# A fused transformer block on one Trainium2 core: whole float32 products for weight tiles without a place, residual sums in single steps, gate columns made later

## The chip, the cores and the metric

The kernel runs on one NeuronCore of a Trainium2 chip. The core has five engines that run side by side, each with its own queue of instructions, worked off in order: TensorE (PE, matrix products; its weight loads are shown as PEld), VectorE (DVE, elementwise work and sums along a row), ScalarE (ACT, functions and copies), GpSimd (POOL) and SyncE (SP, which here only issues transfers). Engines wait for one another through semaphores. The metric is the device time of one execution in microseconds (us), the median of several runs.

## The reference

The block has 256 tokens of 2048 channels and three sublayers: a SwiGLU layer, a mixer (mLSTM heads beside a gated linear recurrence), and a second SwiGLU layer. Each is followed by a residual sum and a layer norm, and preceded by a norm that is modulated with a scale and a shift computed from a conditioning vector:

```python
y = _swiglu(modulate(x, 0), ffn1_w13[l], ffn1_w2[l])
x = _layer_norm(ALPHA * x + FFN_WEIGHT * gate[:, 0, None, :] * y, ln_g[l, 0], ln_b[l, 0])
u = modulate(x, 1)
proj = u @ w_in[l] + b_in[l]
...
x = _layer_norm(ALPHA * x + gate[:, 1, None, :] * y, ln_g[l, 1], ln_b[l, 1])
y = _swiglu(modulate(x, 2), ffn2_w13[l], ffn2_w2[l])
x = _layer_norm(ALPHA * x + FFN_WEIGHT * gate[:, 2, None, :] * y, ln_g[l, 2], ln_b[l, 2])
```

`modulate(x, s)` is a layer norm without affine part, times `1 + scale`, plus `shift`. In the mLSTM, the input and forget gate of four heads give, per token, a running sum of log forget gates and a running maximum; the attention weights of a head are `exp` of differences of these rows. All inputs are float32.

## The kernel before

**Products in three parts.** A float32 product is made of three products in the type fp32r, which TensorE takes faster: every operand is split into a rounded part (hi) and the rest (lo), and hi·hi, lo·hi and hi·lo are summed in PSUM. For a weight tile (128 x 2048, 1 MB, loaded by SP into one of four `raw` buffers) `split` (line 88) makes hi with a cast on ACT (line 95) and lo with a subtraction on DVE (line 97), into one of three hi/lo buffers. `stat_w` (lines 266 to 268) uses the weight as the stationary operand, `mov_t` (lines 277 to 279) as the moving one with 512 columns; activations stand transposed in `uh` and `ul`, 16 blocks of 128 channels by 256 tokens.

**Order.** A planner (the tile framework) orders each engine's queue from a modelled timeline and sets the semaphores. Instructions issued through `V`, `A`, `G` and `T` (class `Pinned`, line 111; all of them are recorded at line 120) keep the order in which the program gives them on DVE, ACT, POOL and PE; all others the planner may move.

**Boundary (line 321).** Between two sublayers the tokens are worked in two tiles of 128 (t = 0, 1). `products(t)` makes the last products of the old sublayer into PSUM tiles `tl`. `take(t, n)` is the residual sum for 512 channels on DVE: product with the gate (`gy`), sum into `x`, row statistics. `norm(t)` is a generator: eight steps on DVE for the layer norm (with row sums), with a square on ACT (`junk`) for each of the last four, then the statistics of the next norm (`tot`, the root on POOL, `nbn` on ACT). `front(t)` makes the next sublayer's input: `n_of` normalises 512 channels, `turned` transposes them on PE into `tu`, `u_of` applies scale and shift (three columns on ACT, one on DVE) and splits the result into `uh` and `ul`, `mov_t` multiplies it with four weight tiles `fw[0..3]` of the next sublayer (`o` after the first boundary, `fg` after the second). `ready` names the tiles of `fw` that find a place (hi/lo buffers or spare slots) before the boundary; the others (`late`) are split in eight or four pieces between the steps of t = 0, hi on ACT, lo on POOL (`late_split`, line 412). At the first boundary (`ffn` of sublayer 0, called at line 1030) tile 3 is late and t = 1 has four residual steps; at the second (end of `mixer`, line 1008) tiles 2 and 3 are late and each t has one.

**Gates (line 804).** In the mixer the projections run over tiles of `w_s`: one tile for the gate rows, 1 to 8 for the recurrence's input (`xr`), 9 to 16 for its output gate (`gg`). `gates()`, called after tiles 1 and 2, makes from the gate rows on DVE a chain of small steps (4 x 256) in the slot `ggt`; its results `gs` and `mt` overwrite two of these rows. `gate_cols()`, called after tile 8, transposes them on PE into `pcol` (lines 819, 820) and copies them to `gcol` and `emc` for the heads. The output gate `gg` is written over the same slot from tile 9 on, by the evacuation at line 759. DVE meanwhile runs the convolution (lines 832 to 836), one product and sum per conditioning tile (line 173, loads `ada`) and the splits `ls`. `rg_gates` (line 838) and `recurrence` (line 848) follow after tiles 12 and 14.

Of the kernel before, what the change touches and what calls it, by code (L numbers as in the profile page):

```python
# [16 lines left out]
P = 128  # L17
# [34 lines left out]
def block_kernel(ctx: ExitStack, tc: tile.TileContext, a: dict, out: bass.AP):  # L52
# [254 lines left out]
    def scaled_by(mv, r, nm):  # L307

        b = sm.tile([P, 1], F32, tag="nb", name="nb" + nm)
        A.mul(b, mv, -1.0)  # L310
        A.activation(b, b, AF.Copy, scale=r)
        return b

# [7 lines left out]
    def boundary(s, ps, hls, order, mm, sts, following):  # L321
# [7 lines left out]
        if following:  # L329
            tiles, nm, ready, in_slots = following  # L330
            fw = [load(tiles[k], f"{nm}{k}", spare if k in in_slots else None) for k in range(4) if k in ready]
        g, b = ln_rows(s)
        if following:
            fw += [load(tiles[k], f"{nm}{k}", None) for k in range(len(fw), 4)]
            late = [k for k in range(4) if k not in ready]
            sb = sm.tile([P, 1], F32, tag="sb", bufs=1, name=f"sb{s}")
# [14 lines left out]
        def low_ahead(k):  # L351
            fw[k] = split(fw[k], nc.scalar, V)

        def norm(t):
# [9 lines left out]
            for n, c in enumerate(cs):  # L364
                if following:
# [3 lines left out]
                    A.activation(junk, x[:, t, c], AF.Square, bias=sb, accum_out=sq[:, 1, n:n + 1])  # L369
# [4 lines left out]
            if following:  # L374
                tot = sm.tile([P, 4], F32, tag="tot", bufs=2, name=f"tot{s}{t}")
                V.tensor_reduce(tot[:, 0:2], sq, op=ALU.add, axis=mybir.AxisListType.X)
                V.tensor_scalar_mul(tot[:, 0:2], tot[:, 0:2], 1.0 / D)
                V.tensor_add(tot[:, 2:3], tot[:, 0:1], sb)

                V.scalar_tensor_tensor(tot[:, 3:4], tot[:, 2:3], tot[:, 2:3], tot[:, 1:2], op0=ALU.mult,  # L380
                                       op1=ALU.subtract)
                r = rstd_in_order(tot[:, 3:4], f"n{s}{t}", -1.0)
                mrb[t] = tot[:, 0:1], r, scaled_by(tot[:, 0:1], r, f"n{s}{t}")
                yield

        def n_of(t, n, k):
            m, r, nb = mrb[t]
            if k == 0:
                V.tensor_scalar(n[:, cs[k]], x[:, t, cs[k]], m, r, op0=ALU.subtract, op1=ALU.mult)
            else:  # L390
                A.activation(n[:, cs[k]], x[:, t, cs[k]], AF.Identity, bias=nb, scale=r)
# [7 lines left out]
        def u_of(t, pt, k):  # L399

            tk = slice(t * P, (t + 1) * P)
            u = sm.tile([P, 4, P], F32, tag="u", bufs=2, name=f"u{s}{t}_{k}")
# [9 lines left out]
        def late_split(k, part):  # L412

            raw, name, _ = fw[k]
            if part == 0:
                lates[k] = [wp.tile([P, 2048], F32R, tag=w, bufs=3, name=w[0] + name) for w in ("hi", "lo")]
            hi, lo = lates[k]
            c = cs[part]
            A.copy(hi[:, c], raw[:, c])
            G.tensor_sub(lo[:, c], raw[:, c], hi[:, c].bitcast(F32))  # L420

        def takes(t, ns):
            for n in ns:
                take(t, n)
                yield
# [6 lines left out]
        def late_pieces():  # L432
            for k in late:
                for part in range(4):
                    late_split(k, part)
                    if part == 3:
                        fw[k] = lates[k]
                    yield

        def front(t, between):  # L440
            n = slot(f"n{s}{t}")[:, 0:D]
            pss.append(bank(f"{nm}{t}"))
            n_of(t, n, 0)
            n_of(t, n, 1)
            pt = [turned(t, n, 0), turned(t, n, 1)]
            for k in range(4):
                between(k)
                u_of(t, pt[k], k)
                if k < 2:
                    n_of(t, n, k + 2)  # L450
                if k:
                    mov_t(pss[t], fw[k - 1], uh, ul, (k - 1) * 4, t, k == 1, False)
                if k < 2:
                    pt.append(turned(t, n, k + 2))
            mov_t(pss[t], fw[3], uh, ul, 12, t, False, True)

        mrb, lates, pss = {}, {}, []
# [14 lines left out]
        A.mul(sb, sb, -1.0 / D)  # L472
        many = len(order[1]) > 1
        other = chain(takes(1, order[1]), norm(1))
        one = norm(0)
        pieces = late_pieces()
        run(one, 8)
        if many:
            run(other, 1)
        run(one)  # L480
        if many:
            run(other, 1)

        def beside(k):
            run(pieces, (0, 2, 2, 0)[k] if len(late) == 1 else 2)
            run(other, (1, 1, 3, 3)[k] if many else (1, 3, 3, 3)[k])

        front(0, beside)
# [636 lines left out]
```

## Time and profile before

| | |
|---|---|
| median of 3 runs | 2036.04 us (2035.77 to 2036.55) |
| the profiled execution | 2036.97 us, span 2035.2 us |
| clock granted to TensorE, mean | 0.981 of full |
| HBM read | 509.22 MB, 251 GB/s over the span |
| first boundary | 801 to 849 us of the span |
| gate columns | 923 to 942 us |
| second boundary | 1236 to 1292 us |

The span is the time between the first and the last instruction of the profiled execution. A profile row of the timeline is: start in us, length in us, engine, line, operation, output and inputs, shapes, count; in brackets the idle time of that engine before it, and what ended it. A row of a group gives count, busy time and mean ns of one, then idle time before. In the waits view a row is engine, line, what it waited for, total us, times, longest.

### The profile page before, as it was taken

The page shows a single profiled execution, that of the slowest core. Times are in us where ns is not written, and L with a number is a line of the kernel's source. Part 1 is how long each engine was busy: PE and PEld are TensorE (multiplying, and loading weights), DVE is VectorE, ACT ScalarE, POOL GpSimd, SP SyncE. Part 2 cuts the span into 40 slices and gives each one's busy share as a digit, 9 for nine tenths or more (in the row PEclk, how much of TensorE's full clock was granted, in tenths as well). Part 3 has the DMA queues.
Part 4 walks back from the last instruction along what each step waited for, and adds up shares of the span by engine and source line. Part 5 has one row for each costly group of instructions (what it writes and reads, how often), then busy time and mean ns, then how long its engine had stood idle before and what let it go on. Part 6 is the DMA issues. An engine that isn't in the chain of part 4 may idle for free.

```text
span 2035.2 us, 30179 instructions
## 1 busy us (share of the span) xinstructions
PE 1952.9 (96%) x13068; PEld 1797.4 (88%) x13068; DVE 1425.5 (70%) x1335; ACT 838.0 (41%) x794; POOL 51.3 (3%) x71
## 2 busy tenths in 40 slices
PE   7899999999999998897999997999999999999997
PEld 6899998799899886697999885899899899899985
DVE  7998898877877757686886886555555544544656
ACT  5433344433334344543744344433433433334340
POOL 0000000000000001100000123000000000000000
PEclk8999999999999999998999998999999999999999
DMA  9998898988988754485687673466666655555552
GB/s 374 349 346 300 307 331 317 349 334 338 358 340 316 264 203 158 159 308 206 237 302 289 223 273 124 170 224 247 237 239 249 227 184 179 189 178 178 187 193 100
DMA packets 72710, 513.27 MB, mean 252 GB/s; under 512 B 8449, under 2 KB 8577, under 8 KB 10881
## 3 DMA queue, kind: packets, MB, share of 16 engines
q1 hardware_dynamic: 70848, 507.54, 67.1%
q10 hardware_dynamic: 1728, 3.80, 0.6%
q8 instruction: 102, 1.67, 0.3%
q14 instruction: 32, 0.25, 0.0%
HBM read 509.22 MB, written 2.10 MB: 251 GB/s over the span
## 4 chain that ended last, share of the span: by engine, by line
PE 86%; DVE 8%; issue 2%; ACT 2%; DMA 2%; POOL 0%; DVEq 0%; SPq 0%; POOLq 0%; ACTq 0%
PE pv L266 6%; PE pv L267 6%; PE pg L268 6%; PE pg L266 6%; PE pv L268 6%; PE pg L267 6%; PE py L278 6%; PE py L279 6%; PE py L277 6%; PE pj L266 2%; PE pj L268 2%; PE pj L267 2%; DVE x L120 2%; PE tl L278 2%; PE tl L279 2%
## 5 line engine op out<-in xcount | busy, mean ns | idle before, releaser
L173 DVE CUSTOM_DVE_ANT_0 ada<-ada,scb,badac 128x2048 f32<-128x2048 f32 x144 | 337.8, 2348 | 31.7 <-DMA ada<-in_w_ada 29.9
L97 DVE TENSOR_TENSOR lw<-rw,hw 128x2048 fp32r<-128x2048 f32 x80 | 183.1, 2290 | 134.2 <-ACT hw L95 134.2
L268 PE MATMUL pg<-uh,lg 128*128 128x256 f32 x960 | 271.8, 283 | 0.0
L268 PE MATMUL pv<-uh,lv 128*128 128x256 f32 x960 | 271.8, 283 | 0.0
L266 PE MATMUL pg<-uh,hg 128*128 128x256 f32 x960 | 271.7, 283 | 0.0
L266 PE MATMUL pv<-uh,hv 128*128 128x256 f32 x960 | 271.7, 283 | 0.0
L267 PE MATMUL pv<-ul,hv 128*128 128x256 f32 x960 | 271.7, 283 | 0.0
L267 PE MATMUL pg<-ul,hg 128*128 128x256 f32 x960 | 271.7, 283 | 0.0
L95 ACT CAST hw<-rw 128x2048 fp32r<-128x2048 f32 x80 | 152.5, 1909 | 214.8 <-PE py L279 63.0
L97 DVE TENSOR_TENSOR lv<-rv,hv 128x2048 fp32r<-128x2048 f32 x68 | 155.7, 2290 | 113.0 <-ACT hv L95 112.9
L95 ACT CAST hv<-rv 128x2048 fp32r<-128x2048 f32 x68 | 129.6, 1906 | 212.6 <-PE pg L267 83.4
L97 DVE TENSOR_TENSOR lg<-rg,hg 128x2048 fp32r<-128x2048 f32 x60 | 137.4, 2291 | 102.1 <-ACT hg L95 102.1
L278 PE MATMUL py<-lw,hth 128*128 128x512 f32 x512 | 203.5, 398 | 2.1 <-DVE lw L97 2.1
L279 PE MATMUL py<-hw,htl 128*128 128x512 f32 x512 | 201.7, 394 | 0.0
L277 PE MATMUL py<-hw,hth 128*128 128x512 f32 x512 | 197.1, 395 | 0.0
L95 ACT CAST hg<-rg 128x2048 fp32r<-128x2048 f32 x60 | 114.3, 1905 | 173.0 <-PE pv L267 115.5
L266 PEld LDWEIGHTS pg<-uh,hg 128*128 128x128 f32 x960 | 183.8, 191 | 0.4
L267 PEld LDWEIGHTS pg<-ul,hg 128*128 128x128 f32 x960 | 183.8, 191 | 0.3
L268 PEld LDWEIGHTS pv<-uh,lv 128*128 128x128 f32 x960 | 183.9, 192 | 0.0
L266 PEld LDWEIGHTS pv<-uh,hv 128*128 128x128 f32 x960 | 183.9, 192 | 0.0
L267 PEld LDWEIGHTS pv<-ul,hv 128*128 128x128 f32 x960 | 183.9, 192 | 0.0
L268 PEld LDWEIGHTS pg<-uh,lg 128*128 128x128 f32 x960 | 183.8, 191 | 0.0
(397 smaller groups left out, 4376.4 us busy)
## 6 DMA issues: line engine op xcount, KB each, us to landing
ada<-in_w_ada SPq DMA_DIRECT2D x144, 1024.0 KB, 5.4
rw<-in_w SPq DMA_DIRECT2D x80, 1024.0 KB, 4.8
rg<-in_w SPq DMA_DIRECT2D x60, 1024.0 KB, 5.0
rv<-in_w SPq DMA_DIRECT2D x60, 1024.0 KB, 4.8
rra<-in_w_r SPq DMA_DIRECT2D x48, 1024.0 KB, 5.5
rs<-in_w_s SPq DMA_DIRECT2D x32, 1024.0 KB, 4.8
rwo<-in_w_out SPq DMA_DIRECT2D x16, 1024.0 KB, 4.8
ro<-in_w_vo SPq DMA_DIRECT2D x8, 1024.0 KB, 4.7
```

What stands on the lines that cost most here:

```text
L95: act.copy(cut(hi, w), like(raw[:, w], hi))
L97: low.tensor_sub(cut(lo, w), like(raw[:, w], lo), cut(hi, w).bitcast(F32))
L120: self.last = getattr(self.engine, op)(*args, **kw)
L173: nc.vector.tensor_tensor_reduce(raw, raw, scb, 1.0, badac[:, s, j, kt:kt + 1], ALU.mult, ALU.add, adac[:, s, j, kt:kt + 1])
L266: nc.tensor.matmul(ps, hi[:, w], uh[:, k0 + j, :], start=st, stop=False)
L267: nc.tensor.matmul(ps, hi[:, w], ul[:, k0 + j, :], start=False, stop=False)
L268: nc.tensor.matmul(ps, lo[:, w], uh[:, k0 + j, :], start=False, stop=sp)
L277: nc.tensor.matmul(o, acth[:, k0 + j, tk], cut(hi, w), start=first and j == 0, stop=False)
L278: nc.tensor.matmul(o, acth[:, k0 + j, tk], cut(lo, w), start=False, stop=False)
L279: nc.tensor.matmul(o, actl[:, k0 + j, tk], cut(hi, w), start=False, stop=last and j == 3)
```

## The change

1. At a boundary the splits of all `ready` tiles are issued before the first residual sum (before, some stood between the sums). The first boundary's tiles are loaded and split in the order 0, 2, 1.
2. `take` yields after each of its three steps, so that `norm` and `take` of the other token tile can be run in single steps; how many steps stand where is written anew (4 per block of t = 0).
3. The statistics after the norm take one DVE step less, and ACT makes the negative mean; a product `sbs` is added.
4. `u_of` uses ACT for all four columns. For a late tile the u of t = 0 is kept whole in float32 in columns of `n0` that are free, and multiplied with the raw weight tile in float32 (`whole_t`: four products of 512 columns). The late weight is split (ACT, DVE) during t = 1, and the whole u is split at the end.
5. The order around the second token tile is new: its first transposes are issued before the last products of t = 0.
6. `gs` and `mt` are written to rows of the slot `misc`, and `gate_cols` is called after tile 14, ahead of `recurrence`; its transposes are pinned.

```diff
-            fw = [load(tiles[k], f"{nm}{k}", spare if k in in_slots else None) for k in range(4) if k in ready]
+            fw = {k: load(tiles[k], f"{nm}{k}", spare if k in in_slots else None) for k in ready}
...
             V.tensor_mul(gy, ps[t, n], gate[:, cs[n]])
+            yield
             V.tensor_add(x[:, t, cs[n]], x[:, t, cs[n]], gy)
+            yield
             V.bn_stats(sts[t][:, n, :], x[:, t, cs[n]])
+            yield
...
-                V.tensor_scalar_mul(tot[:, 0:2], tot[:, 0:2], 1.0 / D)
-                V.tensor_add(tot[:, 2:3], tot[:, 0:1], sb)
+                V.tensor_scalar(tot[:, 2:3], tot[:, 0:1], 1.0 / D, sb, op0=ALU.mult, op1=ALU.add)
...
-                if j < 3:
-                    A.activation(u[:, j, :], pt[:, j * P:(j + 1) * P], AF.Identity, bias=h, scale=m)
-                else:
-                    V.tensor_scalar(u[:, j, :], pt[:, j * P:(j + 1) * P], m, h, op0=ALU.mult, op1=ALU.add)
+                A.activation(u[:, j, :], pt[:, j * P:(j + 1) * P], AF.Identity, bias=h, scale=m)
+            if not whole:
+                split_u(t, u, k)
...
+        def whole_t(ps, raw, u, last):
+
+            for j in range(4):
+                nc.tensor.matmul(ps, u[:, j, :], raw[:, cs[j]], start=False, stop=last and j == 3)
...
-        ahead = list(ready)
-        for i, n in enumerate(order[0]):
-            while ahead and (len(order[0]) == 1 or i == len(order[0]) // 2 or len(ahead) > 2):
-                low_ahead(ahead.pop(0))
-            take(0, n)
+        for k in ready:
+            fw[k] = split(fw[k], nc.scalar, V)
+        run(takes(0, order[0]))
...
+        run(one, 8)
+        run(other, many)
+        run(one)
+        run(other, many)
...
+        un = {k: n0[:, cs[k - 2]].rearrange("p (a b) -> p a b", b=P) for k in late}
+        n_of(0, n0, 0)
+        n_of(0, n0, 1)
+        pt = {}
+        pt[0] = turned(0, n0, 0)
+        pt[1] = turned(0, n0, 1)
...
+        def first(k):
+            if k in late:
+                whole_t(ps0, fw[k][0], un[k], k == 3)
+            else:
+                mov_t(ps0, fw[k], uh, ul, k * 4, 0, k == 0, k == 3)
...
+        for k in range(4):
+            run(other, 4)
+            u_of(0, pt[k], k, un.get(k))
+            if k < 2:
+                n_of(0, n0, k + 2)
+            if k:
+                first(k - 1)
+            if k < 2:
+                pt[k + 2] = turned(0, n0, k + 2)
         run(other)
-        front(1, lambda k: None)
+        n_of(1, n1, 0)
+        n_of(1, n1, 1)
+        pt[0] = turned(1, n1, 0)
+        first(3)
+        pt[1] = turned(1, n1, 1)
+        rest = list(late)
+        for k in range(4):
+            u_of(1, pt[k], k)
+            if k < 2:
+                n_of(1, n1, k + 2)
+            if rest:
+                fw[rest[0]] = split(fw[rest[0]], A, V)
+                rest.pop(0)
+            if k:
+                mov_t(ps1, fw[k - 1], uh, ul, (k - 1) * 4, 1, k == 1, False)
+            if k < 2:
+                pt[k + 2] = turned(1, n1, k + 2)
+        for k in late:
+            split_u(0, un[k], k)
+        mov_t(ps1, fw[3], uh, ul, 12, 1, False, True)
...
-        fc, gs, mx, mt = z4, ig, q4, fg
+        fc, mx = z4, q4
...
+        gs, mt = misc[0:4, 768:768 + S], misc[0:4, 1792:1792 + S]
...
-                nc.tensor.transpose(pcol[:, t * 4:t * 4 + 4], gs[:, t * P:(t + 1) * P], ident[0:4, 0:4])
-                nc.tensor.transpose(pcol[:, 8 + t * 4:12 + t * 4], mt[:, t * P:(t + 1) * P], ident[0:4, 0:4])
+                T.transpose(pcol[:, t * 4:t * 4 + 4], gs[:, t * P:(t + 1) * P], ident[0:4, 0:4])
+                T.transpose(pcol[:, 8 + t * 4:12 + t * 4], mt[:, t * P:(t + 1) * P], ident[0:4, 0:4])
...
-        proj(1, 8, xr, {0: gates, 6: gate_cols})
+        proj(1, 8, xr, {0: gates})
...
-        proj(9, 8, gg, {2: rg_gates, 4: recurrence})
+        proj(9, 8, gg, {2: rg_gates, 4: lambda: (gate_cols(), recurrence())})
...
-    ffn(0, a["w13_1"], a["w2_1"], start, (a["w_vo"][8:12], "o0", (0, 1, 2), (2,)))
+    ffn(0, a["w13_1"], a["w2_1"], start, (a["w_vo"][8:12], "o0", (0, 2, 1), (2,)))
```

More of the change, by code (lines that the diff above doesn't have):

```diff
@@ L304, in scale_x @@
             A.mul(x[:, t, :], x[:, t, :], ALPHA)
[L307 to L312, printed above, removed]
     def rstd_in_order(var, nm, sign=1.0):
@@ L330, in boundary @@
             tiles, nm, ready, in_slots = following
-            fw = [load(tiles[k], f"{nm}{k}", spare if k in in_slots else None) for k in range(4) if k in ready]
+            fw = {k: load(tiles[k], f"{nm}{k}", spare if k in in_slots else None) for k in ready}
         g, b = ln_rows(s)
         if following:
-            fw += [load(tiles[k], f"{nm}{k}", None) for k in range(len(fw), 4)]
             late = [k for k in range(4) if k not in ready]
-            sb = sm.tile([P, 1], F32, tag="sb", bufs=1, name=f"sb{s}")
+            fw.update((k, load(tiles[k], f"{nm}{k}")) for k in late)
+            sbt = sm.tile([P, 2], F32, tag="sb", bufs=1, name=f"sb{s}")
+            sb, sbs = sbt[:, 0:1], sbt[:, 1:2]
         def products(t):
```

73 lines of the change are left out of this document (21 added, 52 removed).

## The prediction

> **What bounds the kernel now.** First the page and the waits of TensorE (engine, line, what it waited for: total us, times, longest).
>
> ```profile
> PE 1952.9 (96%) x13068; PEld 1797.4 (88%) x13068; DVE 1425.5 (70%) x1335; ACT 838.0 (41%) x794; POOL 51.3 (3%) x71
> PE 86%; DVE 8%; issue 2%; ACT 2%; DMA 2%; POOL 0%; DVEq 0%; SPq 0%; POOLq 0%; ACTq 0%
> PE pcol L819 <- DVE gg L810: 13.8, 1, 13.8
> PE tu L120 <- ACT n L120: 10.7, 4, 3.2
> PE fg L277 <- ACT uh L120: 8.6, 3, 4.2
> PE tu L120 <- DVE n L120: 7.9, 3, 5.4
> PE o L277 <- ACT uh L120: 2.6, 2, 1.7
> ```
>
> TensorE is busy 96% of the span and carries 86% of the chain, so only its own idle time can be won. The five longest waits are all in code that the diff touches: the gate columns (13.8 us, once) and the transposes and first products of the two boundaries. The next view is busy time by stage (stretch: length, busy us of PE, PEld, DVE, ACT, POOL, clock), then TensorE's groups inside the two boundaries (the last column is idle time before the group and its releaser).
>
> ```profile
> 801.20:846.50 45.30, 30.19 (x117) 23.21 (x117) 30.11 (x54) 29.03 (x61) 9.76 (x14) 0.81 0.21 73
> 923.00:937.00 14.00, 0.16 (x2) 0.14 (x1) 13.75 (x24) 2.59 (x3) 0.00 (x0) 0.66 0.68 232
> 1235.90:1291.70 55.80, 40.95 (x152) 31.41 (x153) 26.80 (x40) 31.20 (x61) 13.48 (x12) 0.82 0.26 95
> L120 PE MATMUL tu<-ident,n 128*128 128x128 f32 x32 | 6.5, 353 | 12.5 <-DVE n L120 7.7 <-ACT n L120 4.8
> L120 PE MATMUL tu<-ident,n 128*128 128x128 f32 x32 | 5.5, 308 | 6.1 <-ACT n L120 5.9 <-DVE n L120 0.3
> L277 PE MATMUL fv<-hfv,uh 128*128 128x512 f32 x8 | 3.0, 392 | 0.0
> 846.07 0.39 PE L278 MATMUL o<-sl,uh 128*128 128x512 f32 x1
> 846.30 0.40 PE L279 MATMUL o<-sh,ul 128*128 128x512 f32 x1
> 822.28 0.63 PE L277 MATMUL o<-sh,uh 128*128 128x512 f32 x1
> 822.70 0.63 PE L278 MATMUL o<-sl,uh 128*128 128x512 f32 x1
> ```
>
> The first boundary loses 12.5 us before its transposes and 2.6 before its products (o), 15.1 us idle; the second 6.1 and 8.6 (fg), 14.7. On top, after a gap the 512-column products start every 0.42 us (822.28 to 822.70) and not every 0.23 (846.07 to 846.30), with the clock at 0.81 and 0.82 of full.
>
> **Part 1, the gate columns.** Rows in order of time (start, length, engine):
>
> ```profile
> 922.63 0.28 PE L267 MATMUL pj<-ul,hs 128*128 128x256 f32 x1
> 922.75 0.28 PE L268 MATMUL pj<-uh,ls 128*128 128x256 f32 x1
> 926.33 2.27 DVE L97 TENSOR_TENSOR ls<-rs,hs 128x2048 fp32r<-128x2048 f32 x1
> 936.87 0.27 PE L819 MATMUL pcol<-ident,gg 4*128 4x4 f32 x1 [13.84 <-DVE gg L810]
> 937.76 0.41 DVE L813 TENSOR_TENSOR gg<-gg 4x256 f32<-4x256 f32 x1
> 937.87 0.41 PE L266 MATMUL pj<-uh,hs 128*128 128x256 f32 x1
> 938.08 0.41 PE L267 MATMUL pj<-ul,hs 128*128 128x256 f32 x1
> 947.98 2.29 DVE L97 TENSOR_TENSOR ls<-rs,hs 128x2048 fp32r<-128x2048 f32 x1 [5.63 <-ACT hs L95]
> 962.54 1.90 ACT L95 CAST hs<-rs 128x2048 fp32r<-128x2048 f32 x1 [3.82 <-PE pj L267]
> 979.74 1.90 ACT L95 CAST hs<-rs 128x2048 fp32r<-128x2048 f32 x1
> 983.55 2.28 DVE L97 TENSOR_TENSOR ls<-rs,hs 128x2048 fp32r<-128x2048 f32 x1
> 992.40 3.73 PE L144 MATMUL adag<-ident,adac 128*128 128x128 f32 x32
> ```
>
> Tile 8's last product starts at 922.75, the first transpose at 936.87: DVE delivers gs 14 us late. Behind that transpose stand the products of tile 9, although the split of tile 11 (926.33) is done by 928.6. Moved behind tile 14, the four transposes read rows that are final at 938.2 (937.76 + 0.41), long before. The move removes 13.84 us idle and the slow restart: some 18 products at 0.21 us, not 0.12, 1.7 us. Together **15.5 us**. What is late next: tile 9 now runs 922.9 to 928.6 (48 products of 0.12 = 5.76), tile 12 is due at 940.2. Its split stood at 947.98 only because its cast waited behind emc on ACT; in DVE's queue it follows the gate chain, 938.2 + 2.29 = 940.5, so 0.3 us of wait comes back. The evacuations of tiles 9 and 10 overwrite ig and fg, so ACT waits for gs until 936.8, some 2 us that its lead of three tiles hides. Copy gcol and exponential emc move with the transposes and queue before the recurrence. There cover is thin: between the casts at 962.54 and 979.74 ACT has 17.2 us of sigmoids and exponentials, three tiles of TensorE (17.3), and the split behind it ends at 985.8, 0.8 us before tile 16 starts (it ends at 992.40, where the next group begins, so it starts at 986.6). If emc waits there, TensorE pays: 0 to 5 us. The scratch rows cost no instruction. I take **-14.5** (-9 to -16).
>
> **Part 2, the first boundary (801 to 849).**
>
> ```profile
> 781.67 0.69 DVE L120 TENSOR_TENSOR gy<-tl,gate 128x512 f32<-128x512 f32 x1 [5.21 <-PE tl L279]
> 786.55 2.48 DVE L120 TENSOR_TENSOR lo<-ro,ho 128x512 fp32r<-128x512 f32 x4
> 788.95 2.49 DVE L120 TENSOR_TENSOR sl<-ro,sh 128x512 fp32r<-128x512 f32 x4
> 806.62 1.97 PE L120 MATMUL tu<-ident,n 128*128 128x128 f32 x8 [5.40 <-DVE n L120]
> 837.49 0.62 ACT L120 CAST uh<-u 128x512 fp32r<-128x512 f32 x1 [0.48 <-DVE u L120]
> 838.74 1.13 ACT L120 ACTIVATE u<-tu,adac 128x128 f32<-128x128 f32 x3
> 1248.98 1.75 DVE L120 SCALAR_TENSOR_TENSOR x<-x,rsp,ln_b 128x512 f32<-128x512 f32 x1
> 799.20 0.74 DVE L120 SCALAR_TENSOR_TENSOR x<-x,rsp,ln_b 128x512 f32<-128x512 f32 x1
> 962.89 0.59 PE L844 MATMUL pr<-xc,wax 128*128 128x256 f32 x2
> 963.32 0.59 PE L843 MATMUL pr<-xc,wax 128*128 128x256 f32 x2
> ```
>
> (a) *Splits first.* DVE idles 5.21 us ahead of 781.67, and the two 2.5 us splits at 786.55 and 788.95 stand between the residual sums. Put ahead of them they fill the idle time (the third ends near 784.3, after its cast), and the sums run through: the norm starts 3 us earlier. (b) *Single steps.* Two whole takes (three steps of 0.7) stood before and after the row sums of tile 0; now one step each: 2 us. Both together bring the transposes from 806.62 to about 801.4, just behind the last product at 801.2: the 5.40 us gap goes. One scalar step of DVE (0.2 us) goes too; the new product sbs is one ACT step under TensorE's products. (c) *u on ACT alone.* Three columns take 1.13 us, so four 1.5; DVE's fourth column and two handovers go (the cast at 837.49 waited 0.48). Cast and next normalised block take 1.25 more (837.49 to the next u at 838.74), so a block costs ACT 2.8, as much as the 12 products it feeds (12 x 0.23 = 2.8): ACT becomes the pace. (d) *The late tile whole.* The early POOL subtractions go, which cost DVE a doubling (1.75 against 0.74 for one form). Four float32 products replace twelve: a float32 product of 256 columns takes 0.43 (962.89 to 963.32), so 512 columns 0.86 and four 3.4 us, 0.6 more than 2.8. Its split moves to the second block's u, 2.2 us on ACT, 2.5 on DVE, and the late u's cast to the end. Nothing runs on POOL but the square roots.
>
> In order, each engine's queue as the code writes it: transposes 801.4; a gap of 2.4 for u, cast and next block; products of blocks 0 to 2 without a gap to 816.0; two squares of token tile 1 (0.7 each, as all 512-column steps here) delay the late u on ACT to 817.1 (gap 1.1); float32 products to 820.5; second token tile's transposes 820.9, a gap of 2.4, then ACT-paced products to 838.3 (839.3 if the planner puts the float32 products behind those transposes). Idle 6.3 us against 15.1, and one slow restart of about 3. Before, product 846.30 plus tile 3 of token tile 1 (2.8) ends at 849.3. The gain is 10 to 11; a cast of the next weight tile (1.9 on ACT) can fall into the chain: **-10** (-4 to -12).
>
> **Part 3, the second boundary.** One residual step only, so (a) gives nothing and the start stays near 1235.9. Two tiles are late, 4 x 2 float32 products: +1.3 us. POOL's share, and with it DVE's doubled steps, goes. But the code puts a square of token tile 1 ahead of block 1's u, and the statistics of token tile 1 ahead of the two late u: ACT waits 3.0 us for the first and ends the late u near 1252.5 and 1254.0. Gaps of 2.4, 1.7, 1.6 and 2.4 us stay (8 us against 14.7), and restarts stay slow. My queue ends the products at 1275.0 at full clock and 1278.7 with 4 us of 0.42 us starts after each gap over 1.5. Before, they ended with the stretch above, at 1291.5, with a fv tile of 24 products (three groups of 8, 5.6 us) run ahead: 1285.9. Gain 7.2 to 10.9, **-8** (-2 to -11).
>
> [...]
>
> **Sum.** -14.5 - 10 - 8 = -32.5. The profiled execution took 2036.97 (span 2035.2 and 1.8 around it), 0.9 over the median 2036.04: 2004.5 there, **2004** as a median, 1.6% less.
>
> **Rivals.** A, *the gate wait comes back elsewhere*: DVE is busy 13.75 of the 14 us and later must split tiles, copy gcol and run the recurrence in 15 us less; or the transposes are planned early again and wait for mt. For it: the 0.8 us margin; against: DVE's idle at 947.98. 5 to 15 us return: 2009 to 2019, say 2014, 0.17. B, *the clock holds* through the short gaps: parts 2 and 3 come at their full-clock ends, 11 and 10.9: 2000, 0.08. [...] C, *ACT starves the boundaries*: casts of the next tiles and squares sit ahead of u, half of parts 2 and 3 is lost, +9: 2013, 0.10. D, *the raw buffers bind*, the slower side:
>
> ```profile
> rs<-in_w_s SPq DMA_DIRECT2D x32, 1024.0 KB, 4.8
> ```
>
> wax holds one of the four raw buffers until the recurrent gates run and ada tiles another; a load starts only when DVE has done with an earlier tile. If DVE lags so far that one weight tile at a time goes round, load, cast and split in series (4.8 + 1.9 + 2.3 = 9.0 us) replace the 5.76 of its products, 3.2 more per tile. From eleven tiles on the kernel is slower than before; over the 16 tiles from tile 9 through the v projection it is 52 - 32.5, 2055, 0.04. Against it: no wait of TensorE is put down to a load in that stage. E, *the gains are all cover*: TensorE's idle only moves to the following stage: 2036, 0.03.
>
> **How the numbers follow.** Forecast 0.58 (1997 to 2010), A 0.17, B 0.08, C 0.10, E 0.03, D 0.04. The bounds of the three parts taken together, -39 to -15, are 1997 to 2021; they take in A, B and C, and a little below goes to clock and planner: 1995 to 2021, with about 0.13 left out. About 0.2% (4 us) is what a measurement tells from no change: faster 0.93, same 0.03, slower 0.04.
>
> **What would show it.** Part 1: no wait at the transposes, tile 9 straight behind tile 8, pcol after tile 14. Part 2: sums running from 784, transposes near 801, under 7 us of idle to the end of the products. Part 3: three or four gaps of 1.5 to 2.5 us, ACT waiting for the first square. Float32 products at 0.86 us. It is wrong if TensorE waits for ls or lv between 923 and 1040, if the whole products run far over 0.9 us, or if casts break ACT's chain.

## The result, and the profile after

The changed kernel took 2001.79 us (median of 4 runs, 2001.11 to 2003.39), the kernel before, beside it on the same chip, 2036.24 us (4 runs, 2035.77 to 2036.55). The ratio is 0.9832, 95% interval 0.9815 to 0.9849: 34.45 us less, against 32 forecast. The profiled execution has a span of 1999.9 us against 2035.2. Of all executions reported below one, of the changed kernel run again, was slow (2431.24 us at a mean granted clock of 0.726); the ratios leave it out.

First the page of the changed kernel: busy time by engine, and the shares of the chain that ended last.

```profile
PE 1944.2 (97%) x13056; PEld 1785.9 (89%) x13056; DVE 1414.0 (71%) x1327; ACT 843.8 (42%) x812; POOL 36.2 (2%) x59
PE 89%; DVE 6%; ACT 3%; issue 1%; DMA 0%; POOL 0%; DVEq 0%; SPq 0%; ACTq 0%
```

TensorE's share of the chain went from 86 to 89%, DVE's from 8 to 6%: the waits for DVE went, while the work stayed. The waits of TensorE in the changed kernel (engine, line, what it waited for: total us, times, longest):

```profile
PE tu L120 <- ACT n L120: 7.1, 3, 2.4
...
PE fv L277 <- ACT hfv L95: 2.3, 1, 2.3
PE fg L415 <- ACT n L120: 2.3, 1, 2.3
...
PE fv L278 <- DVE lfv L97: 1.6, 2, 1.1
PE tu L120 <- DVE n L120: 1.5, 2, 0.9
PE o L415 <- ACT n L120: 1.3, 1, 1.3
...
PE fg L277 <- ACT uh L120: 1.0, 1, 1.0
```

The 13.8 us for the gate rows are gone, and so are the 5.4 us before the first boundary's transposes. What is left in the boundaries is mostly named ACT: in the rows shown TensorE waits 14.0 us for it (normalised blocks, u, a split) and 3.1 us for DVE. In order of time, TensorE's rows of the first boundary that had idle time before them (start, length, line, tile, in brackets the idle time and its releaser), and the four gate transposes:

```profile
800.66 1.25 PE L120 MATMUL tu<-ident,n 128*128 128x128 f32 x8 [0.59 <-DVE n L120]
804.28 0.66 PE L120 MATMUL tu<-ident,n 128*128 128x128 f32 x4 [2.37 <-ACT n L120]
815.13 3.70 PE L415 MATMUL o<-ro,n 128*128 128x512 f32 x8 [1.31 <-ACT n L120]
819.77 1.25 PE L120 MATMUL tu<-ident,n 128*128 128x128 f32 x8 [0.94 <-DVE n L120]
823.39 1.11 PE L120 MATMUL tu<-ident,n 128*128 128x128 f32 x4 [2.37 <-ACT n L120]
833.74 0.50 PE L278 MATMUL po<-lo,uh 128*128 128x512 f32 x1 [1.08 <-DVE lo L97]
953.64 0.41 PE L120 MATMUL pcol<-ident,misc 4*128 4x4 f32 x4
```

The transposes of the first boundary start at 800.66 and not at 806.62, 0.59 us behind the last products. The gate transposes carry no bracket: TensorE comes to them without a wait. The second boundary, same view:

```profile
1209.20 1.25 PE L120 MATMUL tu<-ident,n 128*128 128x128 f32 x8
1212.82 1.12 PE L120 MATMUL tu<-ident,n 128*128 128x128 f32 x4 [2.37 <-ACT n L120]
1218.57 0.50 PE L277 MATMUL fg<-sh,uh 128*128 128x512 f32 x1 [0.99 <-ACT uh L120]
1224.53 3.70 PE L415 MATMUL fg<-rfg,n 128*128 128x512 f32 x8 [2.25 <-ACT n L120]
1241.73 0.73 PE L277 MATMUL fv<-hfv,uh 128*128 128x512 f32 x2 [2.27 <-ACT hfv L95]
1244.05 0.80 PE L278 MATMUL fv<-lfv,uh 128*128 128x512 f32 x1 [1.07 <-DVE lfv L97]
```

**Where the time came from.** Two executions of the changed kernel differ by a microsecond or two as a whole, those of the kernel before by up to five, so the parts are read from stages: the time between the starts of two TensorE groups that every run has. Stage 1 runs from the first conditioning product `adag` (627 to 629 us) to the first boundary's transposes; stage 2 from there to the `adag` products behind tile 16 (992.40 before), and holds the rest of the first boundary and the gate columns; stage 3 on to the second boundary's transposes; stage 4 from there to the transposes `th` of the second SwiGLU layer (1309.3 before).

| us | stage 1 | stage 2 | stage 3 | stage 4 |
|---|---|---|---|---|
| before | 178.4 | 185.8 | 243.7 | 73.1 |
| changed | 173.6 | 164.9 | 243.6 | 64.8 |
| difference | -4.8 | -20.9 | -0.1 | -8.3 |

Together that is -34.1. Another -1.2 us was there at `adag` already (628.2 before, 627.0 after), though TensorE's order is the same in both kernels up to the first boundary's transposes: runs of the same code spread from 627.0 to 628.8 there, so these 1.2 us are chance.

Stage 2 has a mark inside, the first product of the gate rows, `pif` (its rows before and after: shortest, median and longest in ns, then first and last start):

```profile
L266 PE MATMUL pif<-uh,hif x16: 277/283/283, 871.0 to 876.4; 128*128 128x256 f32 x16
```

```profile
L266 PE MATMUL pif<-uh,hif x16: 278/283/283, 860.2 to 865.6; 128*128 128x256 f32 x16
```

Up to it, in the rest of the first boundary, 64.4 us became 59.6 (-4.8); behind it, with the gate columns, 121.4 became 105.3 (-16.0).

### The profile page after: what moved, and what is told of

Same layout as the page of the kernel before. It is cut to its first block, busy times and chain, and to the rows that moved or that the text cites. A ratio compares the mean times of both kernels' runs of the same rounds, so it can differ in the third digit from the quotient of the medians.

```text
span 1999.9 us, 30155 instructions
## 1 busy us (share of the span) xinstructions
PE 1944.2 (97%) x13056; PEld 1785.9 (89%) x13056; DVE 1414.0 (71%) x1327; ACT 843.8 (42%) x812; POOL 36.2 (2%) x59
## 3 DMA queue, kind: packets, MB, share of 16 engines
q1 hardware_dynamic: 70848, 507.54, 68.6%
## 4 chain that ended last, share of the span: by engine, by line
PE 89%; DVE 6%; ACT 3%; issue 1%; DMA 0%; POOL 0%; DVEq 0%; SPq 0%; ACTq 0%
PE pv L266 6%; PE pg L268 6%; PE pv L267 6%; PE pg L266 6%; PE pv L268 6%; PE pg L267 6%; PE py L278 6%; PE py L279 6%; PE py L277 6%; PE pj L266 3%; PE pj L267 3%; PE pj L268 3%; PE tl L278 2%; PE tl L277 2%; PE tl L279 2%; PE rg L268 2%
```

## The experiments

Twelve kernels, three rounds each with the kernel before beside them (the last two five). The table gives the median, the ratio to the kernel before, and the stages; a dot stands for the value of the changed kernel within 0.1 (stage 3 was 243.6 to 243.8 in all). The stages are those of one profiled execution each.

| run | us | ratio, 95% interval | stage 1 | stage 2 | stage 4 |
|---|---|---|---|---|---|
| gate columns alone | 2019.32 | 0.9924 (0.9909 to 0.9938) | 178.4 | 171.3 | 68.6 |
| boundaries alone | 2015.85 | 0.9909 (0.9894 to 0.9923) | . | 179.5 | 64.6 |
| rows kept, columns early | 2012.80 | 0.9893 (0.9878 to 0.9908) | . | 176.5 | 63.8 |
| u first | 2003.06 | 0.9845 (0.9829 to 0.9862) | . | 166.6 | 62.9 |
| fourth column on DVE | 2011.71 | 0.9882 (0.9868 to 0.9897) | . | 168.7 | 69.8 |
| splits between the sums | 2007.15 | 0.9862 (0.9847 to 0.9877) | 176.7 | 168.3 | 63.7 |
| whole sums | 2005.33 | 0.9849 (0.9833 to 0.9865) | 175.2 | 166.3 | 66.6 |
| late tile split | 2008.15 | 0.9865 (0.9850 to 0.9880) | . | 168.1 | 66.4 |
| gaps filled | 2002.36 | 0.9842 (0.9827 to 0.9856) | . | 165.1 | 63.7 |
| late transposes | 2000.07 | 0.9829 (0.9813 to 0.9846) | . | 164.3 | 63.1 |
| second n on DVE | 1993.80 | 0.9799 (0.9786 to 0.9811) | . | 163.9 | 57.7 |
| changed kernel again | 2001.86 | 0.9836 (0.9823 to 0.9848) | . | . | 63.7 |

Stage 1 repeats within 0.1 us, and so does stage 2 of the changed kernel (164.9 in both of its profiles). The old first boundary does not: up to `pif` it took 64.4 us in the kernel before and 65.9 in the run with the gate columns alone, with the same order of TensorE, DVE and ACT. Stage 4 repeats least: the changed kernel's second boundary, in the same order on every engine, took 63.7 to 66.6 us in six profiles. The old one took 73.1 us, and 68.6 with the gate columns alone; but these two differ in order, since there the planner had put twelve `fg` products of the second token tile ahead of the first `fv` products. In stage 4 only differences of more than 3 us say something.

### Gate columns alone

Part 6 of the change on the kernel before.

```diff
+        gs, mt = misc[0:4, 768:768 + S], misc[0:4, 1792:1792 + S]
...
-        proj(1, 8, xr, {0: gates, 6: gate_cols})
+        proj(1, 8, xr, {0: gates})
...
-        proj(9, 8, gg, {2: rg_gates, 4: recurrence})
+        proj(9, 8, gg, {2: rg_gates, 4: lambda: (gate_cols(), recurrence())})
```

> The kernel before with part 1 alone: gate rows in scratch, gate columns called behind tile 14. Theory (the parts stand alone and add up): the marks of the changed kernel moved by 16 us between pif and the ada product of tile 16, so about 2020 us, no wait of TensorE at the transposes, tile 16 as little late as in the changed kernel. Rival (part 1 got its whole worth only because the first boundary ended earlier and left more cover; alone the wait returns at a split or at emc): 2025 to 2031 us, with a wait for ls, hs or emc's followers between 920 and 1000 us.

Measured 2019.32 against 2035.37 us, 16.1 less; TensorE has no wait at all between 860 and 1120 us. From `pif` to the end of stage 2, 121.4 us became 105.3: 16.0 less, as the medians have it. The other differences between these two profiles (1.5 us more in the first boundary, 4.6 less in stage 4) lie in code that the edit did not touch. The part stands alone; the rival falls.

### Boundaries alone

The changed kernel with these lines taken back, the two transposes unpinned.

```diff
-        gs, mt = misc[0:4, 768:768 + S], misc[0:4, 1792:1792 + S]
...
-        proj(1, 8, xr, {0: gates})
+        proj(1, 8, xr, {0: gates, 6: gate_cols})
...
-        proj(9, 8, gg, {2: rg_gates, 4: lambda: (gate_cols(), recurrence())})
+        proj(9, 8, gg, {2: rg_gates, 4: recurrence})
```

> The changed kernel with part 1 taken back: gate rows in the gate tile, transposes behind tile 8. Theory (parts add up): the 13.8 us wait at the transposes is back, both boundaries stay as in the changed kernel, about 2018 us. Rival (the earlier end of the boundary already brings the gate chain forward, so that the wait shrinks by some us): 2010 to 2014 us, wait under 10 us.

Measured 2015.85, 19.5 less than before. The wait is back, shorter than before (waits of TensorE between 860 and 1120 us):

```profile
PE pcol L826 <- DVE gg L817: 11.3, 1, 11.3
```

Behind `pif` stage 2 takes 119.9 us against the changed kernel's 105.3. So the gate columns are worth 14.5 us where the boundaries are new, and 16.0 where they are old: the parts overlap by 1.5 us, and 16.1 + 19.5 = 35.6 us of the two runs stand against 34.45 for both parts together. The rival had the sign right, though not the size (a wait under 10 us, 2010 to 2014 us). Up to `pif` this run takes 59.6 us, as the changed kernel does, 4.8 less than the kernel before and 6.3 less than the run with the gate columns alone. With stage 1 the first boundary is worth 9.6 us, or 11.1 against that other profile.

### Rows kept, columns early

```diff
-        proj(1, 8, xr, {0: gates})
+        proj(1, 8, xr, {0: gates, 6: gate_cols})
...
-        proj(9, 8, gg, {2: rg_gates, 4: lambda: (gate_cols(), recurrence())})
+        proj(9, 8, gg, {2: rg_gates, 4: recurrence})
```

> The changed kernel with the rows kept in scratch, but the columns made behind tile 8 as before. Theory (the place of the transposes in TensorE's order is what counts, the rows cost and save nothing themselves): the wait at the transposes is back with 12 to 14 us, about 2017 us, same as the run with the rows in the gate tile. Rival (the wait came from the gate tile's reuse by the next evacuations, so that rows of their own remove it wherever the columns are made): 2002 to 2006 us.

Measured 2012.80, between the two. The wait (same view) is 2.7 us shorter than with the rows in the gate tile:

```profile
PE pcol L120 <- DVE misc L818: 8.6, 1, 8.6
```

Most of the gain is the place of the transposes: 11.5 us of stage 2. The rest, 3.0 us of stage 2 against the run with the rows in the gate tile, is there in every execution (2012.01 to 2013.90 us against 2015.18 to 2017.27), but that the rows make it is not shown. Up to the transposes DVE, ACT and TensorE work in the same order in both runs. What differs is DVE's waits for the transfers of conditioning tiles, from 859 us to the transposes (rows in the gate tile, then rows of their own):

```profile
DVE ada L173 <- DMA ada<-in_w_ada: 11.3, 5, 6.1
```

```profile
DVE ada L173 <- DMA ada<-in_w_ada: 8.1, 3, 6.6
```

That is 3.2 us on the engine that makes the gate rows. Why these transfers land later in the one run stays open.

### u first

```diff
         for k in range(4):
-            run(other, 4)
             u_of(0, pt[k], k, un.get(k))
             if k < 2:
                 n_of(0, n0, k + 2)
+            run(other, 4)
```

> The changed kernel with one order changed in the loop over the first token tile's four blocks: u, its cast and the next normalised block are queued before the four steps of the second token tile, so that its squares stand behind u on ACT. Theory (ACT waiting for a square ahead of u makes the gaps of 2.25 and 0.99 us in the second boundary and of 1.31 us in the first): these go, 3 to 5 us less than the changed kernel, 1997 to 1999 us. Rival (DVE is the limit: its steps for the second token tile now wait for ACT's cast and end later, so that the gap moves to the second token tile's first transposes): 2001 to 2004 us, with a wait for n of 3 us or more at those transposes.

Measured 2003.06, no gain. In the changed kernel ACT stood idle for the first square in both boundaries (ACT's rows, first and second boundary):

```profile
813.18 0.72 ACT L120 ACTIVATE junk<-x,sb 128x512 f32<-128x512 f32 x1 [4.15 <-DVE x L120]
1215.65 0.72 ACT L120 ACTIVATE junk<-x,sb 128x512 f32<-128x512 f32 x1 [2.89 <-DVE x L120]
```

With u first the late u's gaps of 1.31, 0.99 and 2.25 us go. In the first boundary the rival holds in kind: the second token tile's transposes then wait 2.39 us for n (0.94 in the changed kernel, 3 or more by the rival), and stage 2 is 1.7 us longer. DVE has 12 steps of residual sums there and must not wait for ACT's cast between them. In the second boundary, with three such steps, stage 4 is 62.9, 0.8 below the lowest of the changed order: a hint, no more.

### Fourth column on DVE

```diff
-                A.activation(u[:, j, :], pt[:, j * P:(j + 1) * P], AF.Identity, bias=h, scale=m)
+                if j < 3:
+                    A.activation(u[:, j, :], pt[:, j * P:(j + 1) * P], AF.Identity, bias=h, scale=m)
+                else:
+                    V.tensor_scalar(u[:, j, :], pt[:, j * P:(j + 1) * P], m, h, op0=ALU.mult, op1=ALU.add)
```

> The changed kernel with the fourth column of every u block back on DVE, as in the kernel before. Theory (the handovers cost more than the column: 0.48 us of wait for DVE's column against 0.38 us of ACT time, and DVE's column queues behind the second token tile's steps): 2 to 6 us more than the changed kernel, 2004 to 2008 us. Rival (ACT is the pace in both boundaries, so a column less on it speeds every block by about 0.3 us): 1998 to 2001 us.

Measured 2011.71, 9.9 more than the changed kernel. The casts of the first three blocks in the first boundary (ACT's rows of this run):

```profile
805.08 0.62 ACT L120 CAST uh<-u 128x512 fp32r<-128x512 f32 x1 [1.08 <-DVE u L120]
...
809.42 0.62 ACT L120 CAST uh<-u 128x512 fp32r<-128x512 f32 x1 [1.96 <-DVE u L120]
...
814.20 0.62 ACT L120 CAST uh<-u 128x512 fp32r<-128x512 f32 x1 [2.40 <-DVE u L120]
```

A column that takes DVE 0.41 us is late by 1 to 2.4 us, since in DVE's queue it stands behind the four steps that this order puts ahead of u. The theory had the sign, but 6 us at most: it priced a handover by the 0.48 us of the old order.

### Splits between the sums, and whole sums

Two runs undo one order each: the splits of the ready tiles back between the sums, and three steps (a whole sum) instead of one at two places.

```diff
-        for k in ready:
-            fw[k] = split(fw[k], nc.scalar, V)
-        run(takes(0, order[0]))
+        ahead = list(ready)
+        for i, n in enumerate(order[0]):
+            while ahead and (len(order[0]) == 1 or i == len(order[0]) // 2 or len(ahead) > 2):
+                k = ahead.pop(0)
+                fw[k] = split(fw[k], nc.scalar, V)
+            run(take(0, n))
```

> The changed kernel with the splits of the ready tiles back between the residual sums of the first token tile. Theory (splits ahead of the sums fill DVE's wait of 5 us, worth 3 us of the first boundary; nothing in the second, which has one sum): transposes of the first boundary 3 us later, about 2005 us. Rival (TensorE's last products end at 800.1 whatever DVE does, and the splits are hidden anyway): 2001 to 2002.5 us.

```diff
-        run(other, many)
+        run(other, 3 * many)
         run(one)
-        run(other, many)
+        run(other, 3 * many)
```

> The changed kernel with three steps instead of one (a whole residual sum of the second token tile) at the two places around the row sums of the first token tile in the first boundary. Theory (four steps of 0.7 us more ahead of the transposes, 0.6 us of it hidden by TensorE's last products): transposes 2 to 3 us later, given back in part by an earlier second token tile (its transposes waited 0.94 us for n): about 2003 us. Rival (what is put off must be done anyway, and the second token tile is late by as much): 2001 to 2002 us, with no wait for n at the second token tile's transposes.

Measured 2007.15 and 2005.33. Stage 1 is 3.1 and 1.6 us longer: 4.7 of the 4.8 us that the change won there. The first transposes of the two runs, in this order:

```profile
803.90 1.95 PE L120 MATMUL tu<-ident,n 128*128 128x128 f32 x8 [3.70 <-DVE n L120]
```

```profile
802.36 1.09 PE L120 MATMUL tu<-ident,n 128*128 128x128 f32 x8 [2.14 <-DVE n L120]
```

Stage 2 grew as well, by 3.4 and 1.4 us. The planner orders the rest of the boundary anew in both; what of the growth is due to that was not taken apart.

### Late tile split

The late tiles split by ACT and DVE behind the u of an earlier block, and multiplied in three products.

```diff
-                whole_t(ps0, fw[k][0], un[k], k == 3)
+                mov_t(ps0, fw[k], uh, ul, k * 4, 0, k == 0, k == 3)
...
+        rest = list(late)
         for k in range(4):
             run(other, 4)
-            u_of(0, pt[k], k, un.get(k))
+            u_of(0, pt[k], k)
+            if rest and k + len(late) > 1:
+                fw[rest[0]] = split(fw[rest[0]], A, V)
+                rest.pop(0)
...
```

> The changed kernel with the tiles without a place split by ACT and DVE before the first token tile's products, which then take three products of 0.23 us per column block and not one in float32 of 0.86 us. Theory (a whole float32 tile costs TensorE 0.6 us more, but saves ACT, the pace of the boundary, 2.2 us of split and 0.6 us of cast ahead of those products): 2 us per late tile, three tiles, 4 to 7 us more than the changed kernel, 2006 to 2009 us. Rival (the split is hidden beside the products of the blocks before, and the float32 products are pure cost): 1999 to 2001 us.

Measured 2008.15, 6.4 more than the changed kernel, as the theory had it; stage 2 is 3.2 us longer. In the second boundary, with two such tiles, TensorE waits 6.29 us for one cast:

```profile
1235.84 0.79 PE L277 MATMUL fg<-hfg,uh 128*128 128x512 f32 x1 [6.29 <-ACT uh L120]
```

### Gaps filled

```diff
+        def fill(t):
+            pf = bank(f"fl{s}{t}")
+            w = fw[0][0]
+            for _ in range(8):
+                T.matmul(pf, w[:, 0:P], w[:, 0:512], start=True, stop=True)
...
         pt[1] = turned(0, n0, 1)
+        fill(0)
...
         pt[1] = turned(1, n1, 1)
+        if many:
+            fill(1)
```

> The changed kernel with eight products of 512 columns whose result nobody reads, put behind the first eight transposes of the first token tile in both boundaries and of the second token tile in the first boundary: 1.8 us of TensorE work inside each gap of 2.4 us. Theory (the products behind such a gap start every 0.42 us only because TensorE stood idle, as in the changed kernel from 824.16 to 826.43 and from 1213.59 to 1215.8): with the gap filled they start every 0.23 us, 2 to 3 us less than the changed kernel, 1999 to 2000 us. Rival (the slow stretches come from the longer lack of full work, transposes and other short gaps too, or the filling work itself runs slowly and delays the transposes behind it): 2001 to 2005 us, with starts of 0.42 us among the filling products.

Measured 2002.36, no gain, yet not for the rival's reason. The filled gap of the first boundary in this run:

```profile
803.25 2.08 PE L120 MATMUL fl<-ho 128*128 128x512 f32 x8
805.87 0.66 PE L120 MATMUL tu<-ident,n 128*128 128x128 f32 x4 [0.53 <-ACT n L120]
```

The gap shrinks to 0.53 us, and the granted clock is 1.00 from 802.2 to 838 (0.95 in the changed kernel; 0.91 in its second profile, from 801.0 on). The slow starts are gone, and stage 2 takes 165.1 us against 164.9 in both of those. So the slow restarts cost the first boundary nothing. Four profiles of the changed boundary say the same: up to `pif` their clocks are 0.97, 0.94, 0.94 and 0.91 (the changed kernel, its second profile, rows kept, boundaries alone), and all four take 59.6 us. That is what is to be expected where TensorE's products wait for ACT anyway.

### Late transposes, and the second token tile's n on DVE

Two steps towards a faster version. First the third and fourth transposes behind the products of a block before, held in this order (products and transposes of both token tiles pinned, in the first boundary the whole products ahead of the second token tile's transposes), and u first in the second boundary only.

```diff
             if k:
                 first(k - 1)
-            if k < 2:
-                pt[k + 2] = turned(0, n0, k + 2)
+            if k in (1, 2):
+                pt[k + 1] = turned(0, n0, k + 1)
...
```

> The changed kernel with two changes in the order: (1) the third and fourth transposes of a token tile behind the products of the first and second block, held in this order, so that the first products wait for the cast of u alone and not for the next normalised block as well (0.8 us of ACT); (2) in the second boundary u ahead of the squares, as in the run with u first, whose second boundary was 1 to 2 us shorter. Theory: 0.7 us at each of four token tiles and 1.5 us in the second boundary, 3 to 5 us less than the changed kernel, 1997 to 1999 us. Rival (ACT is the pace: the transposes that come later hold up the third u, and the gap only moves one block on): 2000 to 2003 us, with a new wait for u or uh at the third block.

Measured 2000.07, which the interval doesn't tell from the changed kernel. The first products start 1.65 us behind the transposes instead of 2.37, yet stage 2 wins only 0.6 us. The wait at the third block that the rival named does not show; in the second boundary the second token tile's transposes now wait 1.65 us for DVE's n. The next step takes ACT's work in the second token tile away:

```diff
-            if k == 0:
+            if k == 0 or t == 1:
                 V.tensor_scalar(n[:, cs[k]], x[:, t, cs[k]], m, r, op0=ALU.add, op1=ALU.mult)
...
-        n_of(1, n1, 0)
-        n_of(1, n1, 1)
+        for k in range(4):
+            n_of(1, n1, k)
```

> The kernel of the run with the late transposes, with all four normalised blocks of the second token tile on DVE (0.55 us each, queued before its transposes) and not three of them on ACT (0.81 us each). Theory (ACT is the pace of the second token tile too, while DVE idles there): 1.6 us less on ACT in each second token tile, together 1 to 3 us less than the run with the late transposes, 1997 to 1999 us. Rival (the casts of the next weight tiles on ACT, 1.9 to 2.2 us each, or TensorE itself set the end there): 2000 us, no difference.

Measured 1993.80, more than expected and clear of all others: 2.0% less than the kernel before (interval 1.9 to 2.1). The changed kernel ran once more beside it:

> The changed kernel itself once more, beside the run with the normalised blocks on DVE on the same chip: 1999 to 2004 us. Its profile shows how far a stage with the same code and the same order of work differs from one execution to the next: by the runs so far 1 to 3 us in the second boundary.

It took 2001.86 us, so n on DVE with the late transposes takes off 8.1 us. Stage 4 fell from 63.1 to 57.7 us, stage 2 by 0.4. Here it is, start to end, in the changed kernel's second profile, with late transposes, and with n on DVE (stretch: length, busy us of PE, PEld, DVE, ACT, POOL, clock); one row for each kernel, in this order:

```profile
1209.50:1273.20 63.70, 54.50 (x217) 39.45 (x218) 33.28 (x43) 41.54 (x73) 2.36 (x4) 0.95 0.42 149
```

```profile
1208.60:1271.70 63.10, 55.57 (x216) 40.44 (x217) 33.26 (x43) 41.38 (x73) 2.37 (x4) 0.92 0.41 150
```

```profile
1208.40:1266.20 57.80, 51.29 (x217) 37.46 (x218) 34.54 (x46) 39.20 (x70) 2.36 (x4) 1.00 0.45 165
```

TensorE's busy time went down by 4.3 us with the same products, and its idle time only by 1.0. With late transposes fv still waits 2.2 us for its split; with n on DVE that wait is gone, the longest in the stage is 1.65 us, and the clock holds. By this pair of executions most of the gain would be a clock that is not lowered. The others do not bear that out: with late transposes executions at mean clocks of 0.991 and 0.992 took 2000.45 and 2000.51 us, with n on DVE 1993.83 and 1993.76 at the same two, 6.6 and 6.8 us less. A mean over the span doesn't say where the clock was low, so how the gain is divided between gap and clock stays open.

## Why the prediction was right, and where it was not

**Part 1 (-14.5, measured -16.0 on the kernel before, -14.5 with the new boundaries).** Right in cause; that the size fits to 0.1 us is luck. The working came to 15.5 us and took 1.0 off for two things that did not happen. The 0.3 us that were to come back did not: TensorE has no wait at all from 860 to 1200 us. And the cover at tile 16 is not thin. DVE's rows of the changed kernel:

```profile
953.25 2.29 DVE L97 TENSOR_TENSOR ls<-rs,hs 128x2048 fp32r<-128x2048 f32 x1 [1.45 <-ACT hs L95]
958.94 0.16 DVE L829 COPY gcol<-pcol 128x8 f32<-128x8 f32 x1
```

Tile 16's split ends at 955.54, ahead of the copy gcol. Tile 15 starts behind the gate transposes at 953.97 and takes 48 products of 0.12 us, so tile 16 starts near 959.7: 4.2 us of cover, not 0.8. That emc would queue ahead of that split was an assumption on the planner's order. What did make part 1 smaller is not in the prediction: with the new boundaries the wait it removes was 11.3 us and no longer 13.8. The 1.5 us that the new boundaries so take off the gate wait are in no part of the forecast, and the sum came out larger by about as much (34.1 by the stages, 32.5 forecast). Rivals A and D had nothing to stand on in this trace.

**Part 2 (-10, measured -4.8 and -4.8 = -9.6; -11.1 against the second profile of the old boundary).** (a) Splits first: 3 us by the working, 3.1 by the run that undid it. (b) Single steps: 2 us by the working, 1.6 measured. (d) A float32 product: eight records in 3.70 us, the last of 0.59, so (3.70 - 0.59) / 7 = 0.44 for half a product, 0.89 for a product against 0.86. The gaps came as listed, 2.37, 1.31 for the late u (1.1), 2.37, and one of 0.94 for n that the queue had not: 7.0 against 6.3. In (c) the size failed. It priced DVE's column at 0.48 us of handover; in the new order the column costs 1 to 2.4 us a block, 9.9 us over the kernel. ACT alone was needed for the rest to work, and not an edit of a few tenths.

**"One slow restart of about 3"** is the step of part 2 that failed. TensorE does restart slowly after one of the two gaps of 2.4 us (starts every 0.43 us from 824.73), but with that removed nothing was won. The working had ACT as the pace already, at 2.8 us a block, and still named the slow products as a loss beside it. It is also not clear on them: rival B's 11 us for a clock that holds is the same end, 838.3 (849.3 - 838.3 = 11.0).

**Part 3 (-8, measured -8.3 in one pair of profiles).** The mean of stage 4 with the changed second boundary (64.8, 64.6, 63.8, 63.7, 66.6, 63.7) is 64.5, which is 8.6 less than the one profile of the old kernel, but 4.1 less than the run with the gate columns alone and its other order (68.6). So the size is no better known than 4 to 9 us. The 4 us of slow starts after each gap over 1.5 were the author's estimate, and no run shows such a rule: in the changed kernel's second boundary slow work behind the first gap, of 2.37 us, lasted 3.0 us (1212.82 to 1215.82), behind the one of 2.25 the clock was 1.00 (1224.5 to 1228.0), and behind the pair of 2.27 and 1.07 products started every 0.43 us for 5.7 us (1244.05 to 1249.77). Of the gaps forecast (2.4, 1.7, 1.6, 2.4) the first three came as 2.37, 0.99 and 2.25. ACT's wait for the first square, 3.0, came as 2.89. The fourth did not, since the second token tile's first four transposes ran between the float32 products, as the code has them, and the other eight behind. In its place stand 2.27 and 1.07 us for fv: the cast of the next weight tile fell between the last u and its cast, which the queue of part 3 did not hold. That the one about makes up for the other (3.3 us against 2.4) is luck.

```profile
1239.78 1.90 ACT L95 CAST hfv<-rfv 128x2048 fp32r<-128x2048 f32 x1
1241.57 0.63 ACT L120 CAST uh<-u 128x512 fp32r<-128x512 f32 x1
```

**The rivals.** B, the clock holds: it did not. Its 2000 us lies nearer to the 2001.79 measured than the forecast's 2004 does, but by luck: what it paid for, a held clock, the run with filled gaps found to be worth nothing in the first boundary, and in the second the clock was low as well (0.92). C, ACT starves the boundaries: right as a bound, wrong as a loss. ACT is what TensorE waits for in both boundaries, and relieving it took off 6.3 us more; but most of its waits were in the forecast's own queue already. E, gains that only move on: stage 3 is the same within 0.2 us, nothing came back there.

## What to carry to other kernels

A wait of a queue worked off in order is best removed by moving the waiting instruction behind work that doesn't need it; the gain was the wait and the slow restart behind it, 16.0 us alone and 14.5 beside the other edits, where the wait was shorter. Once such waits are gone, list what the busiest engine waits for now: here it was ACT, with DVE idle beside it, and moving three normalised blocks of each second token tile from ACT (0.81 us each) to DVE (0.55) brought 6.3 us (2000.07 to 1993.80). Compare stages rather than totals: stages 1 and 3 repeated within 0.2 us where the total spreads over 2. And before a difference is put down to an edit, or to chance, compare the order of the queues and the waits of the engine that makes the late result: two runs here differed by 3 us in the same order, and two stages that looked like repeats were not in the same order.

## What the hardware showed that was not expected

**A gap's length alone doesn't decide how the work behind it runs.** Two gaps of 2.37 us in the changed kernel's first boundary look alike, yet behind the one that ends at 804.28 products start every 0.23 us (granted clock 1.00 from 804.3 to 808.0), and behind the one that ends at 823.39 they start every 0.43 us for a while (0.51 from 823.4 to 826.7). In the kernel's second profile the first of the two, with the same work around it, is followed by slow work as well: its four transposes take 1.12 us and not 0.66.

```profile
804.60 1.12 PE L120 MATMUL tu<-ident,n 128*128 128x128 f32 x4 [2.37 <-ACT n L120]
```

Behind the second gap of that profile, again of 2.37 us, the four transposes take 0.66 us, and starts every 0.43 us come only later, from 824.94 to 827.93. The prediction went by the length, with slow starts after each gap over 1.5 us; what decides beside the length was not shown.

**What a slow stretch cost depended on who set the pace.** In the first boundary, where ACT did, clocks from 0.91 to 1.00 made no difference, as shown above. In the second the same order took 63.7 to 63.8 us at a clock of 0.95 (three profiles), 64.6 and 64.8 at 0.92 and 66.6 at 0.90. TensorE's idle time is 9.2 to 9.5 us in all six, and its busy time 54.3 to 57.4: here the slow products are paid for. The two profiles of the old second boundary can't be set beside each other like this, since their orders differ (the kernel before, then the gate columns alone):

```profile
1236.10:1309.30 73.20, 57.62 (x225) 44.80 (x225) 37.87 (x44) 39.00 (x65) 13.48 (x12) 0.86 0.35 130
```

```profile
1221.60:1290.10 68.50, 54.70 (x224) 43.55 (x225) 37.86 (x44) 38.84 (x65) 13.45 (x12) 0.88 0.37 138
```

DVE and ACT were busy for the same time, TensorE 2.9 us longer and idle 1.8 us longer in the slower one. How much of these 4.7 us is clock and how much order was not taken apart.
